# Tables of a state-space layer stored by group, and a product moved from GpSimd to VectorE

## The chip, the cores and the metric

One core of a Trainium2 chip runs the kernel. The metric is the time of one execution on the device in microseconds. TensorE is called PE here, VectorE DVE, ScalarE ACT, GpSimd POOL and SyncE SP, as in the profile.

## The reference

Two layers of a diffusion backbone over 512 latent tokens and 256 context tokens of 1024 features, in float32: grouped-query attention in the first, a bidirectional state-space layer in the second, a gated feed-forward of 2816 hidden features with a convolution over three tokens after each. What matters here are the matrices of the state-space layer, which hang on parameters alone. For each direction d and each of 64 groups, with 64 complex states n and 16 channels c:

```
dt = exp(log_step);  lb = exp(lam * dt);  bb = (lb - 1) / lam * b
h[t] = lb * h[t-1] + bb @ u[t];   y[t] = Re(c @ h[t])
```

The kernel works by chunks of 8 tokens, so that it wants bb times the powers 0 to 7 of lb (matrix P, from a chunk's inputs to its sum of states), c times the powers 0 to 8 (matrix Q, from a state to a chunk's outputs), and c times powers times bb (the kernel K over lags within a chunk).

## The kernel before, in words

The kernel runs through projections, attention, output projection, feed-forward 0, the state-space layer, its gated unit and feed-forward 1. Products of weights are made of three float32r matmuls (`mm3`, L147 to L149): each chunk of weights of 128x1024 is loaded by SP, ACT copies its high part (L110) and DVE subtracts (L111). The framework orders the instructions of each engine by a simulated timeline (`schedule_with_timeline_sim=True`, L1815); on the chip each engine then runs its list in order.

The matrices of the state-space layer are made as small jobs beside other work, one job at a time:

- `ssm_tables` (L1109 to L1216) runs in attention, a job after each unit of a head and two tiles of tokens. It works out the powers of lb on partitions of (half of the groups, direction, group), copies them twice over into `pd` on POOL (L1186), and turns b, c and the powers to states on partitions: `rows` transposes four of them on PE (L1192), ACT copies them to a staging tile `tst` of two buffers (L1194), and SP stores them (L1196) to the table `tabd` in DRAM, where a row of the table holds 32 groups.
- `ssm_build_in` (L1246) runs in the upward products of feed-forward 0 (`ffn_up`, L845), 18 jobs spread over its blocks 2 to 9 of 22 hidden blocks (with the powers of lambda, L1340 and near, first). For each quarter (half, direction) `table` loads the rows (L1227, L1228) into `tab`, of one buffer, and each of four jobs forms P for eight groups: `products` (L1242 to L1244), transposes on PE (L1261), copies on ACT (L1262), a store by SP (L1263).
- `ssm_build_out` (L1266) does so for Q in 34 jobs over blocks 10 to 20: four groups a job, a store of Q (L1285), a matmul for K (L1290, with columns of the table as weights), its copies (L1293, L1294, L1297, L1298) and four small stores of K (L1302).

The products are elementwise, with a power broadcast over 16 channels and a table row broadcast over the powers. `x` is the table with the groups first, so that its rows lie 32 floats apart:

```
1234  x = tab[:, :, g0:g0 + ng].rearrange("p r g -> p g r")
1239  return (y[:, :, ::-1] if back else y)[:, :, :, None].to_broadcast([P, ng, n, GC])
1241  a, b = (x[:, :, r:r + GC][:, :, None, :].to_broadcast([P, ng, n, GC]) for r in rows)
1242  v.tensor_tensor(t, powers(0), a, op=OP.mult)
1243  nc.gpsimd.tensor_tensor(t2, powers(1), b, op=OP.mult)
1244  v.tensor_tensor(t, t, t2, op=op)
```

P has 8 groups x 8 powers x 16 channels = 1024 elements a partition, Q 4 x 9 x 16 = 576.

In the same blocks of `ffn_up` each upward product (L147 to L149, tile `up`) is followed by its convolution: ACT takes the middle tap out of PSUM (L872), DVE adds two taps (L876, out of PSUM), ACT applies SiLU (L903), DVE multiplies (L904). Until that is done PE can't have the PSUM tile again. Further jobs there (`mods_ahead`, L272) work out modulations: a chunk of weights is scaled by ACT (L295) and added by POOL (L297), or taken by DVE (L299, L301). Weights of both kinds come through five slots of one pool on SP's queue (L206, L823); a slot is free when its chunk was used.

Of the kernel before, what the change touches and what calls it, by code (L numbers as in the profile page):

```python
# [9 lines left out]
FT = mybir.dt.float32  # L10
# [33 lines left out]
ROWS = 50  # L44
R_L = 32
# [11 lines left out]
def spread(runs):  # L57
    """How many of some jobs go with each of the blocks of hidden features; runs: n jobs, for blocks a .. b."""
    return [sum(n * max(0, min(f + 1 - a, b - a)) // (b - a) - n * max(0, min(f - a, b - a)) // (b - a)
                for n, a, b in runs) for f in range(NF)]  # L60


class Weights:
    """Chunks of weights in the order of their use: loaded ahead, and split into two fp32r parts."""
# [69 lines left out]
class Kernel:  # L134
# [16 lines left out]
    def rsqrt(self, pool, ss, n, inv, tag="rs"):  # L151
        """(ss * inv + EPS) ** -0.5 of [P, n]: from a square root and a reciprocal, or, where the
        scalar engine keeps another table, from the exponent's bits, by steps of Newton's."""
# [59 lines left out]
    def mods_rows(self, l, grp):  # L213
        """The bias, and the gain of the norm that the two modulations of a group go with, as rows."""
# [17 lines left out]
    def mods_end(self, l, grp, acc, bg, psum, tag="aux", bufs=2, ms=(0, 1)):  # L232
        """Evacuates a group, stores its rows and, where they are wanted, turns them into columns."""
# [38 lines left out]
    def mods_ahead(self, psum, pool, units, lcs):  # L272
        """Modulations by other engines than the tensor engine, whose sums over partitions alone it takes; as jobs,
        one for each chunk of the weights."""
# [52 lines left out]
    def row(self, pool, l, grp, m, lc, tag, bufs):  # L327
        """A modulation as a row on all partitions."""
# [5 lines left out]
    def transpose_norm(self, psum, work, xn, cols, lc, acts, c0, kps=range(KD // 2)):  # L334
        """Two tiles of tokens, normalised: to features by tokens, modulated, in two parts;
        acts: where tokens lo .. hi go, and the first column there."""
# [23 lines left out]
    def stats(self, x, junk, tag):  # L360
        """x: rows, in one piece or in two; junk: room for their squares."""
# [14 lines left out]
    def plan_proj(self, w, nblk):  # L376
        """w: rows of inputs by columns; in blocks of 512 columns, two blocks of 128 rows a chunk."""
# [5 lines left out]
    def proj_block(self, tiles, act, psum, each, after=None, off=0, out=None, last=False, extra=0):  # L383
        """A block of 512 columns for some tiles of tokens; act: for a block of inputs, its two parts."""
# [38 lines left out]
    def heads(self, t, ps, nh, which, dest, psum, work):  # L423
        """Norm over each head, rotary positions, and the transposition to features by tokens."""
# [35 lines left out]
    def qkv(self):  # L460
# [34 lines left out]
        def load(j):  # L495
            """The weights of the first two modulations of 256 features, then a chunk of the next product's."""
# [37 lines left out]
        def mods(j):  # L534
            """The first two modulations of 256 features, as rows: for either, of each half of the inputs."""
# [7 lines left out]
        def mods_end(j):  # L543
            """To columns, where the halves are summed."""
# [181 lines left out]
    def post(self, *args):  # L726
        """A tile of a sub-layer's outputs: its norm, the gate and the sum with the stream."""
        return self.post_start(*args)()[0]
# [21 lines left out]
    def bank(self, shape, name):  # L750
        """A bank of PSUM for what is soon read, where sums take up two of the three pairs of banks."""
# [14 lines left out]
    def wo(self):  # L766
# [25 lines left out]
        def turn_last():  # L792
            """What the first half of the next layer's tokens doesn't need."""
# [18 lines left out]
    def up_mods(self, l):  # L812
        """How many chunks of modulations go with each of the blocks of hidden features."""
# [18 lines left out]
    def conv_cols(self, l, pool, tmp):  # L832
        """The taps and the bias of the convolution, features on partitions."""
# [275 lines left out]
    def ssm_tables(self, psum, pool, tag, bufs):  # L1109
# [91 lines left out]
        for c in range(0, GC, 4):  # L1201
            rows(c, 4, lambda j: b_of[:, c + j], 1.0)
            yield
# [615 lines left out]
```

## Time and profile before

| | us |
|---|---|
| time, median of 3 runs (lowest, highest) | 1744.71 (1743.69, 1745.6) |
| the profiled execution, by its span | 1744.2 |
| PE busy | 1552.6 (89%) |
| DVE busy | 1166.4 (67%) |
| ACT busy | 772.0 (44%) |
| POOL busy | 373.3 (21%) |

Of the profiled execution the span is known, from the first to the last instruction. Matmuls are pipelined, so that a busy PE is not a PE at its peak. The stages that the change touches are attention (the tables, from 290 to 355 us), and feed-forward 0's upward products, with the jobs of P from 480 to 660 us and those of Q from 677 to 890 us. The granted clock of PE in a stretch is a share of 2.4 GHz; its lower level is 1.2 GHz.

### The profile page before, as it was taken

How to read it: one execution, taken by the hardware profiler on the slowest of the kernel's cores; microseconds unless marked ns; L12 is line 12 of the kernel's file. 1: busy time of each engine (PE TensorE's matmuls, PEld its weight loads, DVE VectorE, ACT ScalarE, POOL GpSimd, SP SyncE). 2: the span in 40 equal slices, each digit the busy share in tenths (PEclk: the TensorE clock that was granted, in tenths of full speed). 3: DMA queues.
4: the chain of work that ended last, by engine and by line, in shares of the span. 5: the costliest groups of instructions: out<-in, count | busy, mean ns of one | idle time of the engine just before them, and what ended most of it. 6: DMA issues, size and time to landing. Idle time of an engine off the chain costs nothing.

```text
span 1744.2 us, 22858 instructions
## 1 busy us (share of the span) xinstructions
PE 1552.6 (89%) x8376; PEld 1247.0 (71%) x8376; DVE 1166.4 (67%) x2036; ACT 772.0 (44%) x1470; POOL 373.3 (21%) x251
## 2 busy tenths in 40 slices
PE   6998489999988888998899999873789999999997
PEld 3775358888867776777788877542568888888886
DVE  4654377768999987888773357689934756565334
ACT  3564256756534333333332245555453534443322
POOL 0111060000255524334410011347501001100000
PEclk8999699999999899999999999886799999999999
DMA  9425181167354546465654269665252424432421
GB/s 308 139 73 170 37 244 47 45 225 256 116 149 136 168 135 198 126 177 179 188 144 163 97 197 273 191 170 183 91 190 85 133 85 145 134 96 97 169 73 48
DMA packets 225445, 256.39 MB, mean 147 GB/s; under 512 B 20621, under 2 KB 176917, under 8 KB 225077
## 3 DMA queue, kind: packets, MB, share of 16 engines
q1 hardware_dynamic: 224900, 254.85, 47.2%
q8 instruction: 66, 1.08, 0.3%
q14 instruction: 47, 0.38, 0.1%
q0 software_dynamic: 384, 0.07, 0.0%
q10 hardware_dynamic: 48, 0.01, 0.0%
HBM read 216.95 MB, written 34.80 MB: 144 GB/s over the span
## 4 chain that ended last, share of the span: by engine, by line
PE 58%; DVE 21%; DMA 8%; issue 5%; ACT 4%; SPq 3%; POOL 2%; DVEq 0%; ACTq 0%; POOLq 0%
PE up L147 6%; PE up L148 6%; PE up L149 6%; PE dn L148 5%; PE dn L147 5%; PE dn L149 5%; DVE whl L111 3%; PE acc L147 2%; DMA wraw<-in_w_mod 2%; PE acc L149 2%; PE acc L148 2%; DVE PT L1242 2%; PE glu L147 2%; PE glu L149 1%; PE glu L148 1%
## 5 line engine op out<-in xcount | busy, mean ns | idle before, releaser
L111 DVE TENSOR_TENSOR whl<-wraw,whl 128x1024 fp32r<-128x1024 f32 x202 | 277.0, 1376 | 176.8 <-ACT whl L110 169.0
L110 ACT ACTIVATE whl<-wraw 128x1024 fp32r<-128x1024 f32 x206 | 216.9, 1056 | 194.8 <-PE dn L149 128.2
L147 PE MATMUL up<-b,whl 128*128 128x256 f32 (+1 forms) x728 | 251.9, 349 | 23.2 <-DVE h L876 18.5
L148 PE MATMUL up<-b,whl 128*128 128x256 f32 (+1 forms) x728 | 249.9, 345 | 0.1
L149 PE MATMUL up<-b,whl 128*128 128x256 f32 (+1 forms) x728 | 249.0, 345 | 0.0
L147 PEld LDWEIGHTS up<-b,whl 128*128 128x128 f32 x728 | 144.0, 199 | 49.1 <-issue 22.6
L148 PE MATMUL dn<-whl,hs 128*128 128x512 f32 x440 | 172.9, 395 | 3.2 <-DVE whl L111 3.1
L149 PE MATMUL dn<-whl,hs 128*128 128x512 f32 x440 | 172.1, 394 | 0.0
L147 PE MATMUL dn<-whl,hs 128*128 128x512 f32 x440 | 170.7, 394 | 0.0
L148 PEld LDWEIGHTS up<-b,whl 128*128 128x128 f32 x728 | 144.4, 199 | 16.9 <-issue 2.1
L149 PEld LDWEIGHTS up<-b,whl 128*128 128x128 f32 x728 | 143.6, 198 | 15.6 <-issue 1.4
L148 PE MATMUL up<-c,whl 128*128 128x512 f32 (+1 forms) x384 | 142.5, 373 | 0.1
L149 PE MATMUL up<-c,whl 128*128 128x512 f32 (+1 forms) x384 | 141.8, 371 | 0.0
L147 PE MATMUL up<-c,whl 128*128 128x512 f32 (+1 forms) x384 | 139.4, 372 | 1.1 <-DVE c L357 1.1
L297 POOL TENSOR_TENSOR macc<-macc,wraw 128x1024 f32<-128x1024 f32 x30 | 87.9, 2930 | 201.3 <-ACT wraw L295 179.5
L876 DVE SCALAR_TENSOR_TENSOR ga<-up,cw,ga 128x511 f32<-128x511 f32 (+1 forms) x132 | 86.7, 657 | 63.9 <-ACT ga L872 62.5
L872 ACT ACTIVATE ga<-up,cw 128x512 f32<-128x512 f32 (+1 forms) x66 | 46.5, 705 | 147.3 <-PE up L149 139.5
L148 PEld LDWEIGHTS dn<-whl,hs 128*128 128x128 f32 x440 | 83.3, 189 | 22.1 <-DVE whl L111 4.1
L876 DVE SCALAR_TENSOR_TENSOR h<-up,cw,h 128x511 f32<-128x511 f32 (+1 forms) x132 | 86.6, 656 | 17.6 <-ACT h L872 16.4
L147 PEld LDWEIGHTS dn<-whl,hs 128*128 128x128 f32 x440 | 83.4, 190 | 19.2 <-ACT ga L872 0.8
L149 PEld LDWEIGHTS dn<-whl,hs 128*128 128x128 f32 x440 | 83.4, 190 | 18.2
L1243 POOL TENSOR_TENSOR QT<-tab 128x576 f32<-128x576 f32 x32 | 66.5, 2079 | 92.6 <-DVE QT L1244 54.0
(358 smaller groups left out, 3294.3 us busy)
## 6 DMA issues: line engine op xcount, KB each, us to landing
wraw<-in_w_up SPq DMA_DIRECT2D x88, 512.0 KB
wraw<-in_w_mod SPq DMA_DIRECT2D x80, 512.0 KB
wraw<-in_w_down SPq DMA_DIRECT2D x66, 512.0 KB
wraw<-in_w_o SPq DMA_DIRECT2D x24, 512.0 KB
Pt<-Pd SPq DMA_DIRECT2D x24, 512.0 KB
Pt<-Qd SPq DMA_DIRECT2D x32, 384.0 KB
wm<-in_w_mod SPq DMA_DIRECT2D x16, 512.0 KB
Pd<-Pb SPq DMA_DIRECT2D x16, 512.0 KB
```

What stands on the lines that cost most here:

```text
L110: nc.scalar.activation(w[:, 0], r, AF.Copy)
L111: e.tensor_tensor(w[:, 1], r, w[:, 0], op=OP.subtract)
L147: nc.tensor.matmul(out, a[0], b[0], start=start, stop=False)
L148: nc.tensor.matmul(out, a[0], b[1], start=False, stop=False)
L149: nc.tensor.matmul(out, a[1], b[0], start=False, stop=stop)
L297: nc.gpsimd.tensor_tensor(a, a, o, op=OP.add)
L872: nc.scalar.activation(o, acc, AF.Identity, scale=c[:, 1:2], bias=c[:, 3:4])
L876: nc.vector.scalar_tensor_tensor(x, acc[:, a + s:b + s], c[:, tap:tap + 1], x, op0=OP.mult, op1=OP.add)
L1242: v.tensor_tensor(t, powers(0), a, op=OP.mult)
L1243: nc.gpsimd.tensor_tensor(t2, powers(1), b, op=OP.mult)
```

## The change

The table becomes three arrays in DRAM (b, c, powers), each with a group's 16 (or 18) values together. `rows` copies into one staging tile for a whole array, of one buffer, and stores the array when it is full: 3 stores instead of 14. The copy `pd` on POOL moves behind the transposes of c and takes the buffer of `ct` (tag "bc") instead of one of its own. `table` loads the powers first into a tile `tabw` of their own. `products` runs its second product on DVE too. The weights of K's matmul are 32 neighbouring columns, so that a group's 16 valid rows lie together and not every second one; the constant `diag16` and the stores of K follow that. Descriptions and headings in the code, which the diff also takes out, are left out here.

```diff
-ROWS = 50
-R_L = 32
...
-        self.tabd = self.dram.tile([P, 4, ROWS, 32], FT, name="tabd")
+        self.tabd = [self.dram.tile([P, 4, 32, n], FT, name=f"tabd{i}") for i, n in enumerate((GC, GC, 2 * TC + 2))]
...
-        pd = pool.tile([P, TC + 1, 2, 2, NS], FT, name="pd")
-        g.tensor_copy(pd, pw[:, :, :, None, :].to_broadcast([P, TC + 1, 2, 2, NS]))
         self.A = self.cst.tile([P, 2, 64], FT, name="lamT")
 
-        def rows(r0, n, src, scale):
+        def rows(i, r0, n, src, scale):
+
+            size = self.tabd[i].shape[3]
+            if r0 == 0:
+                self.whole = pool.tile([P, 4, 32, size], FT, name="tst", tag="tst", bufs=1)
             p = psum.tile([P, 512], FT, name="ptab", tag=tag, bufs=bufs)
             for j in range(n):
                 nc.tensor.transpose(p[:, j * P:(j + 1) * P], src(j), self.ident)
-            st = pool.tile([P, 4, 4, 32], FT, name="tst", tag="tst", bufs=2)
-            nc.scalar.activation(st[:, :, :n].rearrange("p h a b -> p a h b"),
+            nc.scalar.activation(self.whole[:, :, :, r0:r0 + n].rearrange("p h b a -> p a h b"),
                                  p[:, :n * P].rearrange("p (a h b) -> p a h b", a=n, h=4), AF.Copy, scale=scale)
-            nc.sync.dma_start(self.tabd[:, :, r0:r0 + n, :], st[:, :, :n])
+            if r0 + n == size:
+                nc.sync.dma_start(self.tabd[i], self.whole)
             return p
...
         for c in range(0, GC, 4):
-            rows(c, 4, lambda j: b_of[:, c + j], 1.0)
+            rows(0, c, 4, lambda j: b_of[:, c + j], 1.0)
             yield
         for c in range(0, GC, 4):
-            rows(GC + c, 4, lambda j: c_of[:, c + j], sg)
+            rows(1, c, 4, lambda j: c_of[:, c + j], sg)
             yield
+        pd = pool.tile([P, TC + 1, 2, 2, NS], FT, name="pd", tag="bc", bufs=1)
+        g.tensor_copy(pd, pw[:, :, :, None, :].to_broadcast([P, TC + 1, 2, 2, NS]))
         for part in range(2):
             for r in range(0, TC + 1, 4):
                 n = min(4, TC + 1 - r)
-                p = rows(R_L + 9 * part + r, n, lambda j: pd[:, r + j, part].rearrange("p a n -> p (a n)"),
+                p = rows(2, 9 * part + r, n, lambda j: pd[:, r + j, part].rearrange("p a n -> p (a n)"),
                          sg2 if part else 1.0)
...
         nc = self.nc
-        n = 16 * len(sixteens)
-        tab = pool.tile([P, n + 18, 32], FT, name="tab", tag="tab", bufs=bufs)
+        tab = pool.tile([P, len(sixteens), 32, GC], FT, name="tab", tag="tab", bufs=bufs)
+        pws = pool.tile([P, 32, 2 * TC + 2], FT, name="tabw", tag="tabw", bufs=bufs)
+        nc.sync.dma_start(pws, self.tabd[2][:, hd])
         for i, (r, swap) in enumerate(sixteens):
             for a in range(2) if swap else (0,):
                 dst, src = ((slice(64 * a, 64 * a + 64), slice(64 - 64 * a, 128 - 64 * a)) if swap else (slice(0, P),) * 2)
-                nc.sync.dma_start(tab[dst, 16 * i:16 * i + 16], self.tabd[src, hd, 16 * r:16 * r + 16])
-        nc.sync.dma_start(tab[:, n:], self.tabd[:, hd, R_L:])
-        return tab
+                nc.sync.dma_start(tab[dst, i], self.tabd[r][src, hd])
+        return tab, pws
 
     def products(self, tab, g0, ng, n, back, rows, t, t2, op):
-        nc, v = self.nc, self.nc.vector
-        x = tab[:, :, g0:g0 + ng].rearrange("p r g -> p g r")
-        o = x.shape[2] - 18
+        v = self.nc.vector
+        tab, pws = tab
 
         def powers(j):
-            y = x[:, :, o + 9 * j:o + 9 * j + n]
+            y = pws[:, g0:g0 + ng, 9 * j:9 * j + n]
             return (y[:, :, ::-1] if back else y)[:, :, :, None].to_broadcast([P, ng, n, GC])
 
-        a, b = (x[:, :, r:r + GC][:, :, None, :].to_broadcast([P, ng, n, GC]) for r in rows)
+        a, b = (tab[:, r, g0:g0 + ng][:, :, None, :].to_broadcast([P, ng, n, GC]) for r in rows)
         v.tensor_tensor(t, powers(0), a, op=OP.mult)
-        nc.gpsimd.tensor_tensor(t2, powers(1), b, op=OP.mult)
+        v.tensor_tensor(t2, powers(1), b, op=OP.mult)
         v.tensor_tensor(t, t, t2, op=op)
...
-                    lhs = tab.rearrange("p r g -> p (r g)")[:, c:c + 31 * 16 + 1:16]
+                    lhs = tab[0].rearrange("p r g c -> p (r g c)")[:, GC * c:GC * c + 32]
                     nc.tensor.matmul(kp[32 * q:32 * q + 32], lhs, qf[:, q, 16 * d:16 * d + P], start=True, stop=True)
...
-                    x = k[32 * q:32 * q + 32:2, 112:240]
+                    x = k[32 * q:32 * q + GC, 112:240]
```

## Rows read from the trace of the kernel before

**Rows 1.** The page: span, speed of 40 slices, chain by engine.
```profile
span 1744.2 us, 22858 instructions
...
GB/s 308 139 73 170 37 244 47 45 225 256 116 149 136 168 135 198 126 177 179 188 144 163 97 197 273 191 170 183 91 190 85 133 85 145 134 96 97 169 73 48
...
PE 58%; DVE 21%; DMA 8%; issue 5%; ACT 4%; SPq 3%; POOL 2%; DVEq 0%; ACTq 0%; POOLq 0%
```

**Rows 2.** Stretches: from:to, length, busy us by engine, clock, DMA share.
```profile
290.00:355.00 65.00, 62.78 (x478) 58.25 (x477) 49.06 (x125) 47.20 (x110) 0.00 (x0) 1.00 0.17 51
450.00:660.00 210.00, 183.71 (x996) 154.95 (x996) 200.32 (x187) 85.28 (x124) 98.67 (x37) 0.93 0.51 152
660.00:890.00 230.00, 205.53 (x1264) 166.59 (x1264) 187.57 (x234) 73.08 (x124) 95.91 (x45) 0.94 0.60 172
```

**Rows 3.** PE's waits, 440 to 900 us: in all, times, the longest.
```profile
PE up L147 <- DVE h L876: 18.5, 12, 3.1
PE pP L1261 <- DVE PT L1244: 14.5, 8, 3.8
```

**Rows 4.** Groups, 440 to 910 us: busy, mean ns, idle before.
```profile
L297 POOL TENSOR_TENSOR macc<-macc,wraw 128x1024 f32<-128x1024 f32 x26 | 78.3, 3010 | 74.9 <-ACT wraw L295 53.1 <-DVE whl L111 7.9 <-DVE macc L299 7.4
L111 DVE TENSOR_TENSOR whl<-wraw,whl 128x1024 fp32r<-128x1024 f32 x42 | 75.0, 1787 | 2.0 <-ACT whl L110 2.0
L1243 POOL TENSOR_TENSOR QT<-tab 128x576 f32<-128x576 f32 x32 | 66.5, 2079 | 92.6 <-DVE QT L1244 54.0 <-DMA tab<-tabd 35.0 <-DVE Ks L1298 3.6
...
L1243 POOL TENSOR_TENSOR PT<-tab 128x1024 f32<-128x1024 f32 x16 | 46.7, 2920 | 68.4 <-DVE PT L1244 40.9 <-DMA tab<-tabd 14.0 <-DVE ga L876 13.5
```

**Rows 5.** Tiles PT and QT: ns shortest/median/longest, first, last start.
```profile
L1242 DVE TENSOR_TENSOR PT<-tab x16: 2008/2090/4516, 482.5 to 646.3; 128x1024 f32<-128x1024 f32 x16
L1243 POOL TENSOR_TENSOR PT<-tab x16: 2589/2646/4462, 482.8 to 643.0; 128x1024 f32<-128x1024 f32 x16
L1244 DVE TENSOR_TENSOR PT<-PT,PT x16: 1208/1224/3252, 490.6 to 648.5; 128x1024 f32<-128x1024 f32 x16
...
L1242 DVE TENSOR_TENSOR QT<-tab x32: 1168/1244/2625, 677.9 to 885.7; 128x576 f32<-128x576 f32 x32
L1244 DVE TENSOR_TENSOR QT<-QT,QT x32: 741/757/2935, 682.2 to 888.0; 128x576 f32<-128x576 f32 x32
```

**Rows 6.** Timeline (start, length in us), and line L111, 440 to 910.
```profile
455.35 2.11 DVE L1340 TENSOR_TENSOR lpw<-lpw,lpt 128x128 f32<-128x128 f32 x1
...
482.79 4.30 POOL L1243 TENSOR_TENSOR PT<-tab 128x1024 f32<-128x1024 f32 x1 [3.83 <-DVE ga L876]
...
484.84 3.32 DVE L111 TENSOR_TENSOR whl<-wraw,whl 128x1024 fp32r<-128x1024 f32 x1
...
859.67 2.48 DVE L904 TENSOR_TENSOR h<-h,ga 128x512 f32<-128x512 f32 x1 [0.42 <-ACT ga L903]
...
885.70 2.18 DVE L1242 TENSOR_TENSOR QT<-tab 128x576 f32<-128x576 f32 x1
...
L111 DVE TENSOR_TENSOR whl<-wraw,whl x42: 1207/1226/3671, 453.3 to 906.2; 128x1024 fp32r<-128x1024 f32 x42
```

**Rows 7.** Lines with operands far apart or contiguous: ns shortest/median/longest.
```profile
L1631 DVE TENSOR_TENSOR gT<-pg,gT x16: 602/626/697, 1224.8 to 1291.7; 128x256 fp32r<-128x256 f32 x16
...
L1275 DVE TENSOR_TENSOR dmask<-dmask,eye x2: 424/425/426, 673.0 to 785.4; 128x256 f32<-128x256 f32 x2
...
L1630 ACT ACTIVATE gT<-pg x16: 616/644/680, 1224.2 to 1291.0; 128x256 fp32r<-128x256 f32 x16
...
L678 ACT ACTIVATE r<-po x24: 376/385/410, 186.6 to 351.5; 128x256 f32<-128x256 f32 x24
```

**Rows 8.** The copy of the powers, and one of transposes.
```profile
L1186 POOL COPY pd<-pw x1: 2992/2992/2992, 253.7 to 253.7; 128x2304 f32<-128x2304 f32 x1
...
L1194 ACT ACTIVATE tst<-ptab x7: 272/598/634, 290.1 to 341.1; 128x512 f32<-128x512 f32 x6, 128x128 f32<-128x128 f32 x1
```

**Rows 9.** SP queue's waits, 440 to 910 us: in all, times, longest.
```profile
SPq L1285 <- DVE QT L1244: 52.6, 19, 8.1
```

More of the change, by code (lines that the diff above doesn't have):

```diff
@@ L1254, in ssm_build_in @@
                 pt, t2 = (pool.tile([P, 8, TC, GC], FT, name=x, tag=x, bufs=1) for x in ("PT", "PT2"))
-                self.products(tab, 8 * g4, 8, TC, d == 0, (0, GC), pt, t2, OP.add)
+                self.products(tab, 8 * g4, 8, TC, d == 0, (0, 1), pt, t2, OP.add)
                 ptf = pt.rearrange("p g s c -> p g (s c)")
@@ L1282, in ssm_build_out @@
                 t2 = pool.tile([P, 4, TC + 1, GC], FT, name="QT2", tag="QT2", bufs=1)
-                self.products(tab, 4 * gi, 4, TC + 1, d == 1, (GC, 2 * GC), qt, t2, OP.subtract)
+                self.products(tab, 4 * gi, 4, TC + 1, d == 1, (1, 2), qt, t2, OP.subtract)
                 qf = qt.rearrange("p g t c -> p g (t c)")
@@ L1792, in constants @@
             "signs": np.where(np.arange(P)[:, None] < NS, 1.0, -1.0).astype(np.float32),
-            "diag16": (np.arange(P)[:, None] % 32 // 2 == np.arange(GC)[None, :]).astype(np.float32)}
+            "diag16": (np.arange(P)[:, None] % 32 == np.arange(GC)[None, :]).astype(np.float32)}
 _INS = ["x", "c", "ctx", "c_ctx", "w_mod", "b_mod", "g_pre_mix", "g_post_mix", "g_pre_ffn", "g_post_ffn",
```

## The prediction, made before the changed kernel ran

> **What bounds the kernel now.** I read the page first, for the time that all is set against: a span of 1744.2 us [rows 1], 0.5 us under the median of the three runs (1744.71 us), so a difference against the one is a difference against the other. The chain that ended last is PE for 58% and DVE for 21% [rows 1]; DVE's part is where this change works. Then the busy time by stretches, over the three stages that it touches: attention, where the tables are made (290 to 355 us), and the first feed-forward's upward products, under which the input matrices (P, 450 to 660 us) and then the output matrices (Q, 660 to 890 us) are built [rows 2]. In attention PE is busy 62.8 of 65 us, ACT 47, POOL not at all. In the P stage DVE is busy 200.3 of 210 us (95%): it is the limit, and PE idles 26.3 us at a mean granted clock of 0.93 of full speed. In the Q stage DVE has 187.6 of 230 us (82%) and PE idles 24.5 us at 0.94. From the rows PE's own floor is its busy time less what the lower clock level (1.2 instead of 2.4 GHz) took: 183.7 - 0.07 x 210 = 169 us in P, 205.5 - 0.06 x 230 = 192 us in Q. In attention, where PE hardly idles, the same rows show a clock of 1.00. Last, PE's waits: of its idle time most ends with a DVE instruction, a convolution tap (18.5 us, 12 times) or the sum of two products of P (14.5 us, 8 times) [rows 3].
>
> **The change part by part.**
>
> *POOL's product goes to DVE.* POOL loses 48 products, 46.7 + 66.5 us [rows 4], and keeps L297, 26 instructions of 3.0 us. Today a product on POOL makes DVE's next instruction with two SBUF operands long: at 482.79 us L1243 begins and runs 4.30 us, and the split L111 that DVE begins at 484.84 us takes 3.32 us, against a median of 1.23 [rows 6]. I counted, for the stretch 445 to 910 us, the DVE instructions that ran over 0.3 us past the median of their shape and overlapped mostly with a POOL product: 31 with L1243, 45.3 us in excess (14 in P, 27.8 us; 17 in Q, 17.6 us), and 21 with L297, 39.7 us; the first and the last of either are in [rows 6]. The 45.3 us leave with L1243; the 39.7 us stay.
>
> *The products' price.* Today one operand of L1242 is a table read with 128 bytes from row to row, and L1242 takes 2.09 us for 1024 elements and 1.24 us for 576, while L1244, all contiguous, takes 1.22 and 0.76 us [rows 5]. The nearest rows for reading and writing at a distance say the same: L1631, 32 bytes apart, takes 0.63 us for 256 elements where L1275, with a contiguous operand that repeats in a middle dimension, takes 0.42 us [rows 7]. After the change the table rows are contiguous, so I take L1244's price for each of the three: 3 x 1.22 = 3.66 us for 2.09 + 1.22 = 3.31 us in P, 16 times: +5.6 us; 3 x 0.757 = 2.27 for 2.00 us in Q, 32 times: +8.6 us. The lower end of a product is L1244's, the upper L1242's of today, since the other operand (a power, standing still for 16 elements) is in L1242 too and no row shows it alone; I take the lower, because L1631 shows that distance alone slows an instruction. The Trainium skill, page "SBUF — State Buffer", section "Door 1: The DMA port swizzle", says that SBUF is read in lines of 16 bytes and that hits in one line run at full rate; by that a standing operand is free and the sum is as taken. No run here shows that yet.
>
> *What is new to meet L297.* The added DVE time is 16 x 1.22 + 32 x 0.757 = 43.7 us, exposed as the rest is: 39.7 us of excess on 388 us of DVE time [rows 2] is 0.10 us per us, so +4.5 us (2.0 in P, 2.5 in Q). Below it is nothing, above it 48 meetings of 1.9 us (39.7 / 21), 91 us, which would need L297 always to be running; 26 x 3.0 us in 440 us is 18% of the time.
>
> *DVE's balance.* P: -27.8 + 5.6 + 2.0 = -20 us, to 180 us. At the share of 95% that it reaches today the stage takes 180 / 0.954 = 189 us, over PE's floor of 169: **-20 us** (between 0 and -35). Q: -17.6 + 8.6 + 2.5 = -6.5 us, to 181 us. DVE isn't full here, so what counts is which waits of PE go: it loses 24.5 us idle and 14 us by the clock. Waits that a long instruction behind L1243 or a sum L1244 waiting for POOL brought go, those on L297 and on weights stay; I take a third of 38 us, **-12 us** (between -5 and -25). With three products in a row the split, tap or sum queued behind them on DVE waits 1.2 us more in P, 0.8 in Q; that is inside the DVE sums.
>
> *Table loads and SP.* The loads are as many and as large as before (16 rows of 32 floats were 2 KB in one piece, 32 groups of 16 are), the powers now first: nothing. SP's queue holds the stores of P and Q and the weights behind them; it waits for the sums L1244 (52.6 us in all, 19 times [rows 9]), which now come earlier.
>
> *The stores of the tables, in attention.* Fourteen stores become three of 1 to 1.15 MB, each at its table's end, and the one staging tile is single: ACT's first copy into the next table waits for the store of the last. ACT writes with 64 to 72 bytes between elements instead of rows of 32: L1630, writing 32 bytes apart, takes 0.64 us for 256 elements where L678 takes 0.39 [rows 7], so the twelve copies of 512 elements (0.60 us the median [rows 8]) gain up to 0.5 us each, 6 us on an engine with 18 us of slack in 65. The POOL copy of the powers (2.99 us [rows 8]) moves behind the last transposes of c, whose buffer it takes; PE's transposes of the powers come right after it. POOL has nothing else there. Cover for all this is PE's other attention work, which the scheduler can put in front; without it the price is 3 us for the copy, 3.4 us for each of two stores that are waited for (1 MB at 308 GB/s, the fastest slice of the page [rows 1]), and 6 us for ACT: 16 us. And the last store puts 1.15 MB instead of 64 KB ahead of the next loads on SP's queue. I take **+3 us** of 0 to 16.
>
> *Ks and pK.* Each of 64 stores leaves 16 neighbouring partitions instead of every second of 32, and the weights of pK are contiguous. Nobody waits for these stores before the state-space layer reads them, but for the buffer; 0 to +3 us, taken as 0.
>
> Sum: -20 - 12 + 3 = -29 us on 1744.2, or **1716 us** against the median.
>
> **Rivals.**
>
> *Relief that is not used* (chance 0.16): POOL's L297 gets longer where three DVE products run in a row, as L1243 did behind L1242 (4.30 us at 482.79 us [rows 6] for the usual 2.65 [rows 5]); its weight slot comes free later and the weights behind it on SP come late. Speaks for it: L297 stays the cause of 40 us of excess. Against: it no longer queues behind 113 us of products. Half of P's gain and none of Q's: -10 + 3, 1738 us. The Trainium skill, same page, section "Who interferes with whom", has the rule that such a pair excludes each other for a whole instruction, whoever issues first; the trace agrees with the 4.30 and the 3.32 us.
>
> *All of PE's stalls go* (0.18): with DVE no longer late the clock stays up too, and both stages come near PE's floors: at the full -41 and -38 us 1669 us, half-way from the forecast 1692 us. Against: L297 and waits for weights remain.
>
> *The standing operand is what is slow* (0.10; the other side): a product stays at 2.09 and 1.24 us. Then DVE gains 2.09 x 16 = 33 us in P and 1.24 x 32 = 40 us in Q, less 27.8 and 17.6, plus 7 for L297: +9 us in P, all on the path, and +26 us in Q, of which half shows: +22 + 3, 1770 us. It decides from a product of 1.9 us in P and 0.9 us in Q on (where 2x plus the sum is today's price plus the relief). Against: L1631.
>
> *It does not do what it says* (0.05): the distance was not what the reads cost or the scheduler spends the relief; no change, 1744 us.
>
> **How the numbers follow.** The forecast (1702 to 1729 us) has 0.51. From 1684 to 1742 us lie it, the unused relief, and most of the case of PE's floor: 0.8. About 0.2% (3.5 us) is what a measurement here can tell from no change. Faster: 0.51 + 0.18 + 0.16 = 0.85; same 0.05; slower 0.10.
>
> **What would show it.** Right: no POOL product of PT or QT; three DVE products at about 1.22 and 0.76 us; the mean of L111's splits down from 1.79 us in this stretch [rows 4] to about 1.4; DVE's busy time in P near 180 us and the stage some 20 us shorter; the rest of the kernel as long as before. Wrong: the two products near 2.1 us (the standing operand); an idle PE at 306 to 312 and 326 to 332 us behind ACT or POOL (stores and copy); L297 well over 3.0 us and PE waiting as long as before (unused relief).

## The result: 1725.8 us against 1745.2

The changed kernel takes 1725.78 us (median; 1721.58 to 1729.18) against 1745.15 us of the kernel before beside it: a ratio of 0.9885, 95% interval [0.9868, 0.9902], 19.4 us less. Run again as e0, it had 1724.31 against 1746.83 us, 0.9869 [0.9848, 0.9891], 22.5 us less. The forecast was 29 us less, with a range that holds it.

The page of the changed kernel: span, busy time by engine, chain by engine, to be set beside [rows 1].

```profile
span 1723.6 us, 22808 instructions
...
PE 1531.6 (89%) x8376; PEld 1230.2 (71%) x8376; DVE 1132.2 (66%) x2084; ACT 776.6 (45%) x1470; POOL 252.3 (15%) x203
...
PE 64%; DVE 16%; DMA 10%; ACT 5%; issue 3%; SPq 3%; POOL 0%; DVEq 0%; ACTq 0%; POOLq 0%
```

DVE's share of the chain falls from 21 to 16%, DMA's rises from 8 to 10%. DVE's busy time over the whole kernel falls although it has 48 instructions more: before it was 1166.4 us (x2036). POOL's falls from 373.3 us.

The stretches of [rows 2], after:

```profile
290.00:355.00 65.00, 61.01 (x459) 55.99 (x458) 48.97 (x119) 49.94 (x106) 2.11 (x1) 1.00 0.08 33
450.00:660.00 210.00, 191.31 (x1104) 163.54 (x1103) 188.45 (x224) 91.89 (x134) 46.18 (x21) 0.97 0.53 156
660.00:890.00 230.00, 209.86 (x1300) 166.76 (x1299) 183.60 (x284) 78.30 (x133) 29.27 (x13) 0.96 0.67 181
```

PE does more in the same time (996 matmuls became 1104) at a higher granted clock (0.93 to 0.97). But a fixed stretch holds more work in a faster kernel, so its 188 us of DVE can't be compared with the old 200. I therefore cut the stage by work: at its first upward product, at the middle of its 2184 matmuls, and at the last. The stretches view of the kernel before, cut so:

```profile
421.50:665.30 243.80, 216.30 (x1274) 186.60 (x1274) 226.24 (x262) 105.19 (x162) 100.37 (x38) 0.94 0.50 151
665.30:922.60 257.30, 232.83 (x1400) 188.45 (x1398) 204.67 (x261) 82.83 (x140) 94.92 (x45) 0.95 0.56 162
```

and of the changed kernel:

```profile
425.90:654.10 228.20, 208.37 (x1273) 181.10 (x1272) 203.34 (x279) 105.73 (x164) 42.83 (x19) 0.97 0.52 155
654.10:898.20 244.10, 223.96 (x1384) 179.21 (x1383) 193.23 (x294) 82.28 (x138) 32.74 (x16) 0.97 0.66 176
```

With the same matmuls in each half (1274 and 1273; a few records more or less in the second), the first half, where P is built, is 15.6 us shorter and the second, with Q, 13.2. The first down product follows 246.9 us after the middle before and 235.0 after, 11.9 us less. With the stage's start 4.4 us later and the rest of the kernel 2.5 us longer, that is the whole difference: -15.6 - 11.9 + 4.4 + 2.5 = -20.6 us, from a span of 1744.2 to 1723.6. Only half of the first half's gain is idle time of PE (27.5 to 19.8 us): PE's busy time for the same matmuls also falls, by 7.9 us (216.30 to 208.37), with the granted clock at 0.97 after 0.94.

The products, after: tile PT, then QT (shortest/median/longest ns), beside [rows 5].

```profile
L1243 DVE TENSOR_TENSOR PT<-tabw,tab x16: 1209/1214/3067, 486.7 to 645.7; 128x1024 f32<-128x1024 f32 x16
L1244 DVE TENSOR_TENSOR PT<-tabw,tab x16: 1207/1214/2755, 490.8 to 640.2; 128x1024 f32<-128x1024 f32 x16
...
L1243 DVE TENSOR_TENSOR QT<-tabw,tab x32: 737/750/2947, 672.3 to 870.1; 128x576 f32<-128x576 f32 x32
L1244 DVE TENSOR_TENSOR QT<-tabw,tab x32: 736/746/2848, 673.9 to 868.3; 128x576 f32<-128x576 f32 x32
L1245 DVE TENSOR_TENSOR QT<-QT,QT x32: 740/747/2552, 675.0 to 870.8; 128x576 f32<-128x576 f32 x32
```

A product takes what a sum takes. The longest of each line, 2.6 to 3.4 us, met a POOL sum. The groups of POOL's sums and of the splits, 440 to 910 us, beside [rows 4] (lines 297 and 111 are now 295 and 109); the mean of the splits falls from 1787 to 1390 ns, as forecast (1.4 us):

```profile
L295 POOL TENSOR_TENSOR macc<-macc,wraw 128x1024 f32<-128x1024 f32 x26 | 71.5, 2749 | 185.1 <-ACT wraw L293 119.1 <-DVE Ks L1299 56.0 <-DVE macc L299 5.1
L109 DVE TENSOR_TENSOR whl<-wraw,whl 128x1024 fp32r<-128x1024 f32 x45 | 62.6, 1390 | 8.6 <-ACT whl L108 8.6
```

PE's waits, beside [rows 3], in the same stretch as there:

```profile
PE up L145 <- DVE h L874: 15.9, 9, 5.1
PE up L145 <- DVE ga L874: 10.9, 6, 3.8
...
PE pP L1262 <- DVE PT L1245: 2.7, 2, 1.6
```

The wait for the sum of P fell from 14.5 to 2.7 us; those for the convolution's taps did not fall in all (18.5 + 4.6 before, 15.9 + 10.9 after). DVE now waits for table loads in P, which it did not before, and longer in Q:

```profile
DVE PT L1244 <- DMA tab<-tabd: 9.4, 3, 5.0
...
DVE QT L1243 <- DMA tab<-tabd: 7.8, 4, 4.1
```

In the kernel before, DVE had one such row, and POOL's product bore most of these waits (14.0 + 35.0 us [rows 4]):

```profile
DVE QT L1242 <- DMA tab<-tabd: 4.7, 2, 2.5
```

### The profile page after: what moved, and what is told of

Read it like the earlier page. It is cut to its first block, busy times and chain, and to the rows that moved or that the text cites. A ratio compares the mean times of both kernels' runs of the same rounds, so it can differ in the third digit from the quotient of the medians.

```text
span 1723.6 us, 22808 instructions
## 1 busy us (share of the span) xinstructions
PE 1531.6 (89%) x8376; PEld 1230.2 (71%) x8376; DVE 1132.2 (66%) x2084; ACT 776.6 (45%) x1470; POOL 252.3 (15%) x203
## 4 chain that ended last, share of the span: by engine, by line
PE 64%; DVE 16%; DMA 10%; ACT 5%; issue 3%; SPq 3%; POOL 0%; DVEq 0%; ACTq 0%; POOLq 0%
PE up L145 8%; PE up L146 8%; PE up L147 8%; PE dn L146 5%; PE dn L145 5%; PE dn L147 5%; DMA wraw<-in_w_mod 2%; PE acc L145 2%; PE acc L146 2%; PE acc L147 2%; DMA tab<-tabd 2%; DVE whl L109 2%; PE glu L145 2%; PE glu L147 1%; PE glu L146 1%
## 5 line engine op out<-in xcount | busy, mean ns | idle before, releaser
L109 DVE TENSOR_TENSOR whl<-wraw,whl 128x1024 fp32r<-128x1024 f32 x202 | 259.8, 1291 | 178.3 <-ACT whl L108 176.8
L145 PE MATMUL up<-b,whl 128*128 128x256 f32 (+1 forms) x728 | 248.5, 343 | 27.8 <-DVE h L874 15.9
L146 PE MATMUL up<-b,whl 128*128 128x256 f32 (+1 forms) x728 | 246.7, 340 | 0.1
L147 PE MATMUL up<-b,whl 128*128 128x256 f32 (+1 forms) x728 | 246.4, 340 | 0.0
L145 PEld LDWEIGHTS up<-b,whl 128*128 128x128 f32 x728 | 140.8, 194 | 51.8 <-issue 31.1
L146 PEld LDWEIGHTS up<-b,whl 128*128 128x128 f32 x728 | 141.1, 194 | 18.9 <-issue 4.3
L147 PEld LDWEIGHTS up<-b,whl 128*128 128x128 f32 x728 | 141.0, 194 | 16.7 <-issue 2.4
L295 POOL TENSOR_TENSOR macc<-macc,wraw 128x1024 f32<-128x1024 f32 x30 | 81.1, 2704 | 312.1 <-ACT wraw L293 246.2
L874 DVE SCALAR_TENSOR_TENSOR h<-up,cw,h 128x511 f32<-128x511 f32 (+1 forms) x132 | 86.2, 653 | 19.0 <-ACT h L870 18.5
L145 PEld LDWEIGHTS up<-c,whl 128*128 128x128 f32 x384 | 71.4, 188 | 15.1 <-DVE c L355 1.5
```

The lines of the kernel that those rows point to most:

```text
L109: e.tensor_tensor(w[:, 1], r, w[:, 0], op=OP.subtract)
L145: nc.tensor.matmul(out, a[0], b[0], start=start, stop=False)
L146: nc.tensor.matmul(out, a[0], b[1], start=False, stop=False)
L147: nc.tensor.matmul(out, a[1], b[0], start=False, stop=stop)
L295: nc.gpsimd.tensor_tensor(a, a, o, op=OP.add)
L874: nc.vector.scalar_tensor_tensor(x, acc[:, a + s:b + s], c[:, tap:tap + 1], x, op0=OP.mult, op1=OP.add)
```

## The experiments

Each time stands beside the kernel before on the same chip (ratio and its 95% interval). The halves are those cut by work above. DVE and POOL are busy times over the whole kernel. Halves and busy times are of the one profiled execution, which need not be the median one. "Early" means tables loaded in halves, ahead of use.

| run | layout | second product | other | median us | ratio | first half | second half | DVE | POOL |
|---|---|---|---|---|---|---|---|---|---|
| before | old | POOL | | 1745.2 to 1746.8 | 1 | 243.8 | 257.3 | 1166.4 | 373.3 |
| e0 | new | DVE | the change | 1724.31 | 0.9869 [0.9848, 0.9891] | 226.8 | 246.6 | 1129.1 | 252.0 |
| e1 | new | POOL | | 1723.49 | 0.9865 [0.9847, 0.9882] | 229.0 | 243.2 | 1115.4 | 330.2 |
| e2 | old | DVE | | 1751.94 | 1.0024 [1.0014, 1.0033] | 237.7 | 260.1 | 1184.9 | 258.7 |
| e3 | new | DVE | early | 1715.63 | 0.9824 [0.9807, 0.9842] | 227.2 | 234.9 | 1134.4 | 251.1 |
| e10 | new | POOL | early | 1707.14 | 0.9774 [0.9756, 0.9792] | 225.7 | 229.3 | 1111.4 | 334.6 |
| e9 | old | POOL | early, 64-byte pieces | 1748.40 | 1.0009 [1.0, 1.0019] | 230.1 | 263.0 | 1152.8 | 357.3 |
| e13 | old | POOL | early, whole pieces | 1739.98 | 0.9965 [0.9951, 0.9979] | 231.5 | 254.0 | 1153.0 | 359.2 |
| e7 | new | DVE | early, evictions in order | 1712.53 | 0.9810 [0.9790, 0.9831] | 226.9 | 236.4 | 1134.4 | 253.0 |
| e8 | new | DVE | early, no POOL modulations | 1701.06 | 0.9746 [0.9721, 0.9771] | 216.5 | 230.4 | 1127.4 | 170.1 |
| e12 | new | DVE | early, their sums on DVE | 1700.21 | 0.9747 [0.9727, 0.9768] | 218.0 | 231.4 | 1119.8 | 170.0 |
| e11 | new | POOL | as e8 | 1698.82 | 0.9729 [0.9716, 0.9741] | 213.3 | 227.5 | 1112.1 | 248.1 |

### The change again, and its two parts alone

The changed kernel, unedited:

> The changed kernel as it is, beside the kernel before on one chip: the yardstick of the runs sent with it. Every theory expects its measured ratio again, 0.985 to 0.991 (some 1726 us).

It came to 0.9869, as expected. The layout alone:

```diff
-        v.tensor_tensor(t2, powers(1), b, op=OP.mult)
+        self.nc.gpsimd.tensor_tensor(t2, powers(1), b, op=OP.mult)
```

> The layout of the change with the second product back on POOL: tables by group, contiguous rows, but DVE has two products of a matrix and POOL one. My theory (the gain comes from two things, the slow second product taken from POOL with its contention on DVE, and the shorter first product): half of it, 1730 to 1740 us; the upward-product L109 group's mean stays near 1.6 to 1.8 us, and DVE again loses 30 to 45 us beside the POOL product. Rival (the layout alone makes the gain, by the shorter first product and weight loads): 1722 to 1730 us. Rival (the engine alone makes it): 1741 to 1748 us.

It took 1723.49 us, no worse than the whole change. My theory of two halves fell; the rival that the layout alone makes the gain held. Why, two tile rows of this run and a group row (430 to 890 us) show:

```profile
L1244 POOL TENSOR_TENSOR PT<-tabw,tab x16: 1942/2014/2955, 485.8 to 628.9; 128x1024 f32<-128x1024 f32 x16
...
L1244 POOL TENSOR_TENSOR QT<-tabw,tab x32: 1167/1177/2093, 665.7 to 858.2; 128x576 f32<-128x576 f32 x32
...
L1244 POOL TENSOR_TENSOR QT<-tabw,tab 128x576 f32<-128x576 f32 x32 | 42.5, 1327 | 83.4 <-DVE QT L1245 56.2 <-DMA tab<-tabd 20.7 <-DVE Ks L1299 6.4
```

POOL's own product gets shorter too: the median from 2646 [rows 5] to 2014 ns for P, and for Q the mean from 2079 [rows 4] to 1327 ns. Counted as in the prediction (410 to 920 us), its excess on DVE is 25.7 us in 26 pieces, where it was 45.2 us in 31. So a good part of the 45.3 us that were to leave with L1243 goes with the layout, while the product stays on POOL. With DVE's own first product, shorter by (2.09 - 1.22) x 16 + (1.24 - 0.75) x 32 = 29.6 us, that is 49 of the 51 us by which DVE's busy time falls (1166.4 to 1115.4). The layout is a bundle, though: its stores, the loads' order and the weight loads of K's matmul (mean 148 to 110 ns, 256 of them) change with it, and no run takes these apart. The Trainium skill, page "GPSIMD Engine Reference", section "7. Performance pitfalls for Q7 kernels", says of custom kernels on this engine that a read whose step is over 8 bytes costs about half as much again. This product is no custom kernel; here the old rows stood 128 bytes apart, and 2646 against 2014 ns is 31% more: the same direction, a smaller size.

The engine alone, in the old layout (the same line of the kernel before):

```diff
-        nc.gpsimd.tensor_tensor(t2, powers(1), b, op=OP.mult)
+        v.tensor_tensor(t2, powers(1), b, op=OP.mult)
```

> The kernel before with the second product on DVE, old layout: DVE takes 16 more products of some 2.1 us and 32 of some 1.24 us, 73 us in all, and loses the 45 us of contention. My theory: DVE is then later for its upward products and P tiles by the difference, and the time is 1745 to 1765 us, slower than before. Rival (taking POOL's product away is the whole gain, the layout does nothing): 1722 to 1730 us. Rival (the second product's slow operand is not slow on DVE): under 1730 us with products of 1.2 us.

It is slower, 1751.94 us, as expected. Its tile rows show both products at the old price:

```profile
L1242 DVE TENSOR_TENSOR PT<-tab x16: 2004/2093/4204, 485.0 to 651.1; 128x1024 f32<-128x1024 f32 x16
L1243 DVE TENSOR_TENSOR PT<-tab x16: 2007/2054/4075, 488.5 to 647.2; 128x1024 f32<-128x1024 f32 x16
```

DVE's busy time rises by 18.5 us. The first half is 6.1 us shorter (PE waits 4.3 us for sums of P, where it waited 14.5), the second 2.8 us longer; there PE waits for sums of Q, 11.9 us where it was 3.6:

```profile
PE pK L1290 <- DVE QT L1244: 11.9, 8, 3.5
...
PE pP L1261 <- DVE PT L1244: 4.3, 2, 2.4
```

With e1 this settles the split: the layout is worth 23 us with the product on POOL (1746.83 to 1723.49) and 28 us with it on DVE (1751.94 to 1724.31); moving the product costs 5 us in the old layout and, within the intervals, nothing in the new.

### What makes an operand slow

36 products of 128x1024 elements added at the kernel's end, whose results go nowhere; the time of this run (1735.28 us, once) is not compared with others.

```diff
+            v.tensor_tensor(out, full, full, op=OP.mult)
+            v.tensor_tensor(out, wn, full, op=OP.mult)
+            v.tensor_tensor(out, wo, full, op=OP.mult)
+            v.tensor_tensor(out, full, rn, op=OP.mult)
+            v.tensor_tensor(out, full, r4, op=OP.mult)
+            v.tensor_tensor(out, full, r8, op=OP.mult)
+            v.tensor_tensor(out, full, ro, op=OP.mult)
+            v.tensor_tensor(out, wo, ro, op=OP.mult)
+            v.tensor_tensor(out, wn, rn, op=OP.mult)
```

> The changed kernel with 36 DVE products of 128x1024 at its end, four each of nine forms: both operands plain; the repeated power from the new table or from the old one (128 bytes from row to row); the row of sixteen contiguous, 16, 32 or 128 bytes apart; both old; both new. Theory (a read whose elements lie far apart costs, a repeated one doesn't): 1.21 us for all but the rows 32 and 128 bytes apart, which take 2.0 to 2.1 us, alone or with the old power; the row 16 bytes apart is open, 1.2 or 2.1 us. Rival (the repeated power is slow): the forms with it take 2 us, with a plain second operand too. Second rival (it takes both old operands): only the form with both old takes 2.1 us.

The tile view, its rows in the order of the diff (w: repeated power, r: row of sixteen; n: new, o: old table; r4, r8: 16 and 32 bytes apart):

```profile
L1794 DVE TENSOR_TENSOR mout<-mfull x4: 1214/1216/1269, 1374.6 to 1454.9; 128x1024 f32<-128x1024 f32 x4
L1795 DVE TENSOR_TENSOR mout<-mpws,mfull x4: 1218/1220/1271, 1378.9 to 1457.8; 128x1024 f32<-128x1024 f32 x4
L1796 DVE TENSOR_TENSOR mout<-mold,mfull x4: 1216/1244/2781, 1381.9 to 1459.6; 128x1024 f32<-128x1024 f32 x4
L1797 DVE TENSOR_TENSOR mout<-mfull,mnew x4: 1214/1217/2832, 1383.7 to 1464.1; 128x1024 f32<-128x1024 f32 x4
L1798 DVE TENSOR_TENSOR mout<-mfull,ms x4: 1974/1987/1995, 1385.4 to 1466.5; 128x1024 f32<-128x1024 f32 x4
L1799 DVE TENSOR_TENSOR mout<-mfull,ms x4: 2027/2088/2157, 1388.5 to 1471.4; 128x1024 f32<-128x1024 f32 x4
L1800 DVE TENSOR_TENSOR mout<-mfull,mold x4: 1961/2058/2094, 1391.2 to 1474.7; 128x1024 f32<-128x1024 f32 x4
L1801 DVE TENSOR_TENSOR mout<-mold x4: 2058/2088/2141, 1393.8 to 1479.1; 128x1024 f32<-128x1024 f32 x4
L1802 DVE TENSOR_TENSOR mout<-mpws,mnew x4: 1209/1219/1273, 1397.6 to 1482.9; 128x1024 f32<-128x1024 f32 x4
```

The repeated power is free from either table (1.22 and 1.24 us); a row whose elements stand 16 bytes apart or more costs 2.0 to 2.1 us by itself, and the second old operand adds nothing. The theory held; the open case, 16 bytes, is slow.

### The table loads

Early tables in the changed kernel: half the groups to a load, in two buffers of half the size, asked for one matrix job ahead in P and three in Q (shown: the tiles, and the part for P).

```diff
-        tab = pool.tile([P, len(sixteens), 32, GC], FT, name="tab", tag="tab", bufs=bufs)
-        pws = pool.tile([P, 32, 2 * TC + 2], FT, name="tabw", tag="tabw", bufs=bufs)
+        tab = pool.tile([P, len(sixteens), 16, GC], FT, name="tab", tag="tab", bufs=2)
+        pws = pool.tile([P, 16, 2 * TC + 2], FT, name="tabw", tag="tabw", bufs=2)
...
-            tab = self.table(pool, hd, ((0, False), (0, True)), 1)
             for g4 in range(4):
+                if hd == g4 == 0:
+                    tabs = [self.table(pool, 0, 0, ((0, False), (0, True)))]
+                if g4 % 2 and (hd, g4) != (3, 3):
+                    tabs.append(self.table(pool, hd + g4 // 2, 1 - g4 // 2, ((0, False), (0, True))))
+                tab = tabs[2 * hd + g4 // 2]
```

> The changed kernel with the tables loaded in halves of sixteen groups, in two buffers of half the size, each half asked for three steps ahead of its first product. In the changed kernel DVE waits 19.5 us for table loads that POOL's product bore before. My theory (a part of what fell short of the forecast is these waits, which hold back the modulations and hidden features that stand behind them on DVE): the waits fall under 5 us and the time falls by 5 to 10 us, to 1716 to 1721 us. Rival (the waits are hidden, PE has other work then): within 2 us of the changed kernel, with the waits gone.

1715.63 us, 8.7 us less by the medians; the waits for tables are down to 1.8 us. So far my theory held, but not in its place. The stretches, cut by work:

```profile
424.20:651.40 227.20, 207.00 (x1274) 180.49 (x1273) 205.61 (x280) 106.19 (x164) 42.47 (x19) 0.95 0.51 155
651.40:886.30 234.90, 224.10 (x1393) 181.06 (x1391) 193.46 (x292) 82.28 (x139) 33.42 (x16) 0.97 0.67 185
```

The first half, where DVE had waited 11.1 us for tables, is as long as before the edit; the 9 to 12 us came in the second. The same with the product on POOL (the edits of e3 and e1 together):

> The changed kernel with half tables in two buffers, asked for ahead (as in the run of that), and with the second product back on POOL. With the product on DVE the early tables gave 8.7 us (1724.3 to 1715.6). My theory (the waits for tables cost only where all products stand on DVE in order; a POOL product bears them in its own idle time): from 1723.5 of the layout with POOL to 1719 to 1724 us, less than half of that gain. Rival (whoever has the second product, the matrix is late by the load, so the early tables give 7 to 11 us here too, and the kernel before paid for the loads as well): 1712 to 1717 us. Second rival (POOL also gains its 48 us of waits, and DVE is freer by 22 us of products): under 1711 us.

1707.14 us, 16 us under e1: my theory, that a POOL product bears the loads in idle time, fell, and the time lies where the second rival put it. Whoever multiplies, the early loads gain; why 16 us here and 9 us in e3 isn't shown. It also means that with early tables the move to DVE costs: e3 is 8.5 us above e10, with intervals that don't meet (0.9807 to 0.9842 against 0.9756 to 0.9792). All this raised the question whether the kernel before had paid for the loads as well. The same early halves in its old layout:

> The kernel before, in its old layout and with POOL's product, with the tables loaded in halves of sixteen groups, in two buffers, asked for ahead. With the new layout early tables gave 8.7 us where DVE had the second product and 16.4 us where POOL had it. Theory A (table loads cost nothing before the change: POOL's 49 us of waits for them were idle time, and the loss came with the order on DVE): 0 to 4 us, 1742 to 1748 us. Theory B, which I now hold for likelier (a matrix is late by its load whoever multiplies, so the kernel before paid for the loads too, and the change did not bring that cost): 9 to 17 us, 1729 to 1738 us. If B holds, the tables do not explain why the change fell short of the forecast.

1748.40 us, nothing gained, which looks like theory A. But half of an old row is 64 bytes, and the page of that run counts 340676 packets where the page of before has 224900:

```profile
q1 hardware_dynamic: 340676, 254.86, 51.2%
```

The second half was 263.0 us, longer than before. In the profile the whole stage is even so 5.5 us shorter up to the first down product (490.7 to 485.2), but starts 1.0 us later, and the rest of the kernel is 5.0 us longer. So the tables were stored by halves too, and the loads read 1 KB in one piece:

```diff
-        self.tabd = self.dram.tile([P, 4, ROWS, 32], FT, name="tabd")
+        self.tabd = self.dram.tile([P, 4, 2, ROWS, 16], FT, name="tabd")
...
-            nc.sync.dma_start(self.tabd[:, :, r0:r0 + n, :], st[:, :, :n])
+            for q in range(2):
+                for h in range(4):
+                    nc.sync.dma_start(self.tabd[:, h, q, r0:r0 + n], st[:, h, :n, 16 * q:16 * q + 16])
```

> The kernel before with early half tables again, but with the tables in DRAM stored by halves, so that a half table's load reads whole stretches (16 rows of 16 groups, 1 KB) and no pieces of 64 bytes: the run before it had 340,676 DMA packets where the kernel before has 224,900, and a DMA share of 0.68 in the stage against 0.54, so it was no clean test of the loads. The cost moves to the stores of the tables in the attention stage, 64 bytes a piece, once. Theory A (in the old layout the loads are not what the stage waits for): 0 to 4 us, 1742 to 1748 us, as with the short pieces. Theory B (the kernel before paid for the loads too, and the short pieces hid it): 7 to 17 us, 1729 to 1740 us.

1739.98 us, 6.6 us less (interval 3.7 to 8.6): between the two theories. In its profile the stage is 14.4 us shorter up to the first down product (490.7 to 476.3):

```profile
425.50:657.00 231.50, 208.94 (x1274) 181.01 (x1273) 215.36 (x264) 104.87 (x162) 93.41 (x38) 0.96 0.52 155
657.00:911.00 254.00, 229.20 (x1394) 184.96 (x1392) 200.34 (x260) 82.82 (x140) 89.12 (x45) 0.95 0.59 167
```

and it starts 4.0 us later, behind the smaller stores of the tables; the rest of the kernel, which no edit touches, is 4.8 us longer than in the profile of before. So the kernel before paid for its table loads too, mostly in P, where the changed one pays in Q, and by the time (6.6 against 8.7 us) about as much. The loads are then not what the change lost, as far as these two runs tell, whose intervals leave room for a few us.

### What is left on POOL, and the evictions

POOL's share of the modulations (an ACT scaling and the POOL sum L295) as one DVE instruction each, on top of e3's edit:

```diff
-                    if lc == lcs - 1 and (lc or k % 2):
-                        o = w if k else a
-                        nc.scalar.activation(o, w, AF.Copy, scale=c)
-                        if k:
-                            nc.gpsimd.tensor_tensor(a, a, o, op=OP.add)
-                    elif k == 0:
+                    if k == 0:
```

> The changed kernel with half tables in two buffers, and POOL's share of the modulations (an ACT scaling and the POOL sum L295, 26 in this stage) as one DVE instruction each. DVE takes 26 more of some 1.25 us, 33 us, and loses the 42 us by which the POOL sum lengthens its work; ACT loses 26 scalings. My theory (DVE's work in the stage sets the time): 9 us less work on DVE, 1709 to 1716 us against 1715.6. Rival (only the order of the waits counts, POOL's sums are harmless): within 2 us of it, or over it by up to 10 us, as DVE's own queue grows.

1701.06 us, 14.6 us under e3, more than the theory's 6.6 at most. The splits now run undisturbed (410 to 920 us):

```profile
L109 DVE TENSOR_TENSOR whl<-wraw,whl 128x1024 fp32r<-128x1024 f32 x61 | 74.2, 1217 | 30.3 <-ACT whl L108 30.3
```

To see whether ACT's relief did it, ACT keeps its scalings here and only the sums move to DVE:

```diff
-                            nc.gpsimd.tensor_tensor(a, a, o, op=OP.add)
+                            v.tensor_tensor(a, a, o, op=OP.add)
```

> The changed kernel with early half tables, ACT's scaling kept and the sum of POOL's share of the modulations on DVE: 26 sums of some 1.22 us come to DVE and 42 us of contention go, with ACT's work as in the changed kernel. Moving scaling and sum to DVE gave 14.6 us (1715.6 to 1701.1). Theory (contention on DVE is what the sums on POOL cost): 1700 to 1706 us. Rival (ACT's relief is the gain): 1711 to 1717 us.

1700.21 us, the same as e8 with ACT's work as in e3 (777.6 us busy), so ACT's relief is not the gain: it comes with taking the sums off POOL. Between their excess on DVE (40 to 44 us in e3 and e7, by how the shapes are grouped) and weights held until a slow sum is done, these runs don't choose. Then e8 with the second product on POOL (the line of e1):

> The new layout with early half tables, the second product on POOL and POOL's share of the modulations on DVE, as one instruction each. DVE's work in the stage comes to some 440 us, 21 less than with the second product on DVE (461) and about as much as with both on POOL (442). Theory (DVE's work in the stage sets the time, and POOL's product costs it 22 us of contention against 43 us of products): 1690 to 1700 us. Rival (what the modulations gained was ACT's relief of 30 us of scalings and POOL's late sums, and a product on POOL brings its hand-over back): 1700 to 1707 us.

1698.82 us, the fastest of all, 27 us under the changed kernel's first median, though not told apart from e8 and e12 by its interval. It lies in the theory's range, but 1.2 us from the rival's, so that it doesn't decide between them; and here the place of the second product, 8.5 us with POOL's sums in place, makes no difference that can be told.

Last, e3 with the evictions of the transposed tables written in the staging's own order:

```diff
-            nc.scalar.activation(self.whole[:, :, :, r0:r0 + n].rearrange("p h b a -> p a h b"),
-                                 p[:, :n * P].rearrange("p (a h b) -> p a h b", a=n, h=4), AF.Copy, scale=scale)
+            nc.scalar.activation(self.whole[:, :, :, r0:r0 + n],
+                                 p[:, :n * P].rearrange("p (a h b) -> p h b a", a=n, h=4), AF.Copy, scale=scale)
```

> The changed kernel with half tables in two buffers, and the nine evictions of the transposed tables by ACT written in the staging's own order (half, group, row) instead of row by row. In the changed kernel each takes 1.12 to 1.17 us against 0.60 before. Theory (the write of single elements 64 bytes apart is the slow side): 0.6 to 0.9 us each, and the first upward product 1 to 3 us earlier than in the changed kernel's run on this chip. Rival (the order doesn't matter, or the read at 512 bytes apart is as slow): 1.1 us or more, the stage as late as before. The time: 1712 to 1716 us or 1715 to 1718 us.

The tile view shows them at the old price (in the changed kernel the medians are 1062 and 1184 ns, before 598 [rows 8] and 689):

```profile
L1193 ACT ACTIVATE tst<-ptab x7: 409/598/672, 291.5 to 347.0; 128x512 f32<-128x512 f32 x6, 128x128 f32<-128x128 f32 x1
L1193 ACT ACTIVATE tst<-ptab,sg x7: 497/687/832, 311.9 to 358.0; 128x512 f32<-128x512 f32 x6, 128x128 f32<-128x128 f32 x1
```

But the first upward product starts at 425.1 us, no earlier (424.2 us in e3): the evictions are hidden. The 3 us between the medians of e7 and e3 lie within their intervals.

## Why the forecast was right, and 7 to 10 us too large

*POOL's product goes to DVE* was the step that failed as a reason. It put all of the 45.3 us of contention down to where the product runs. e1 shows the same time with the product left on POOL; the layout shortens POOL's product as well, which the prediction never priced, and nearly half of the contention goes with that. The move takes the other 25.7 us and the hand-overs between DVE and POOL away, but DVE is busy 14 us more in the end (1115.4 to 1129.1): in this kernel it comes out even. The sum's total survived because layout and move were costed together.

*The products' price* was right: 1.21 us and 0.75 us for 1.22 and 0.757. Choosing the lower end because distance alone is slow is what e6 confirms by itself, and the rival of the standing operand fell. L1631 had not shown it: it also reads an operand out of PSUM, which L1275 doesn't. By the passage of the Trainium skill cited in the prediction (page "SBUF — State Buffer", section "Door 1: The DMA port swizzle") a standing operand is free: e6 agrees, 1.220 us against 1.216.

*What is new to meet L297*: +4.5 us lies among what can be counted, and no nearer can it be told. Over 410 to 920 us, against the median of DVE instructions of the same operation and shape, POOL's sums cost DVE 34.6 us in 20 pieces before and 42.8 in 24 after, +8; other groupings of the shapes give +2 to +10, and 39.7 us was one such count. By the first, 6.7 of the 8.2 us came before 660 us, in P, where 2.0 was forecast.

*DVE's balance* is where the size went, in P. DVE's work there fell by 22.9 us (226.24 to 203.34), even more than the 20 us forecast. But "at the share of 95% that it reaches today" did not hold: cut by work, DVE was busy 92.8% of the first half before (226.24 of 243.8) and 89.1% after (203.34 of 228.2). At the old share the half would be 219 us, 24.7 us shorter; it became 15.6. A freed engine began to wait: for tables 11.1 us in this half and for modulation weights 5.9.

```profile
DVE macc L299 <- DMA wraw<-in_w_mod: 5.9, 3, 3.3
```

Taking the table waits away (e3) only let other waits come up, for ACT (5.7 and 4.6 us):

```profile
DVE h L874 <- ACT h L870: 5.7, 6, 1.9
DVE ga L874 <- ACT ga L870: 4.6, 5, 1.6
```

What did shorten this half was taking POOL's sums away (227.2 to 216.5 in e8, 218.0 in e12). Q's -12 us was met, -11.9, but its reason was thin: no row stood behind the third of PE's stalls, and DVE's work in the second half fell by 11.4 us (204.67 to 193.23), where 6.5 was forecast for Q. That the two agree is in part luck.

*Attention*, +3 us, was about right: the stage started 4.4 us later in the first profile and 3.1 in e0. Over nine profiles with the new tables the first upward product is at 424.2 to 426.2 us, mean 425.1, over the three with the old tables and stores (before, e2, e9) at 421.5 to 423.7, mean 422.6. The evictions are not its cause (e7); store and copy were not tried apart.

*Table loads: nothing* held as a difference (e13 against e3), though not because loads are free. *Ks and pK: 0* met no row that speaks against it, but was not tested: the weight loads of K's matmul did get shorter. The remaining 2.5 us lie behind the first down product, where the change edits nothing: 832.0 us in the profile of before, 834.5 after, 832.0 to 839.1 in the others, in no order.

So of 8.4 us by which the profiled change fell short (29 against 20.6), 4.4 are P, 1.4 attention, 2.5 the scatter of the rest. Of the rivals, the relief that is not used needed longer POOL sums; their mean fell from 3010 to 2749 ns. The case of no change fell by the interval. That all of PE's stalls go fell too: PE idles 19.8 us of the first half and 20.1 of the second, after 27.5 and 24.5.

## What to carry to other kernels

Price a new layout on every engine that reads it, the one that the change takes the work from as well, and test each part of a two-part change alone: here the layout was all of it, on DVE and on POOL. Where an engine's busy time falls, don't keep its busy share: it will start to wait for what had been hidden behind it, so look for the next wait, and compare stages cut at the same work, not at the same time. Moving an elementwise product off POOL pays only if it costs DVE less than the hand-over and contention that it takes away; here that was even in the changed kernel, a loss of 5 us in the old layout and of 8.5 us with early tables, while taking POOL's other sums, 2.7 us each, to DVE was worth 15 us.

## What the runs showed of the hardware that was not expected

- A DVE product of 1024 elements takes 1.22 us with a row operand that is contiguous and 1.99 us with its elements only 16 bytes apart; 32 or 128 bytes are hardly worse (2.09, 2.06), and two such operands cost no more than one (2.09).
- A POOL product reading contiguous rows takes 2.01 us instead of 2.65 (1024 elements).
- Halving the loads' pieces to 64 bytes raised the packets from 224900 to 340676 and the DMA share of 410 to 920 us from 0.54 to 0.68, with no more bytes (254.86 MB); with 1 KB pieces it was 0.56.
